# LayerNorm tile by tile, one activation table set for its root, and the first gate chunks multiplied tile by tile

## The chip, the cores and the metric

The kernel runs on one core of a Trainium2 chip. The metric is the device time of one execution in microseconds; three runs of the kernel before gave 2117.9, 2118.01 and 2118.44 us, and their median is what the changed kernel is compared with. The engines are named as the profile names them: PE multiplies matrices (PEld is its weight loading), DVE and ACT work on whole tiles element by element (ACT also evaluates functions such as the logarithm, from tables that an ACT_TABLE_LOAD brings in), POOL is a third elementwise engine, and SP issues most of the DMAs. Each engine executes its own instructions in order and waits for the others by semaphores.

## What is computed

A two-layer decoder trunk over 512 tokens of width 2048. Each layer has a mixer (sparse attention in layer 0, stick-breaking attention in layer 1), and after it the same tail, which is the only part that the change touches:

```
for i in range(DEPTH):                                   # DEPTH = 2
    y = mixer_i(x, ...)                                  # ends with a product with w_out
    x = _layer_norm(DN_ALPHA * x + y, ln_g[i], ln_b[i])  # (x - mu) * rsqrt(var + eps) * g + b
    x = x + (p[i] @ w_ple[i]) * jax.nn.sigmoid(x @ w_ple_gate[i])
```

All arithmetic is float32. The normalised x is the input of the product with `w_ple_gate`, so no gate product can start before the LayerNorm has delivered at least its first tile.

## The kernel before, in words

Activations lie transposed: a tile is 128 features by 512 tokens, and the residual stream is 16 such tiles, here tile 0 to tile 15. To keep float32 accuracy on PE, every factor is split into a high part (a rounded copy, written by ACT) and a low part (the difference, written by DVE), and a product is three matmuls of 512 columns: high weight by high tile (L120), high weight by low tile (L121), low weight by high tile (L122), in `mm3`. The high part of a tile is needed at the first of these, its low part at the second.

Weights come as chunks of 128x1024 numbers (512 KB), one DMA each into one of six `raw` buffers. `split_w` turns a chunk into `wh` (ACT, L294) and `wl` (DVE, L295); there are three pairs of `wh`/`wl` buffers (`HL_BUFS = 3`), and the split of chunk c is issued two chunks ahead, at the start of chunk c-2. `Kernel.run` goes through the list of chunks in order: first `ahead(c)` (splits and loads due), then the chunk's multiplications, then its `after` function, then deferred work. So the place of a call in this list is the place of its instructions in every engine's queue. PSUM gives four banks for products (tag `g`).

The tail of a layer consists of these chunks:

- 32 chunks of `w_out`, which end in the 16 unnormalised tiles `z` and in running sums for the statistics.
- Four `ple` chunks, the product with `w_ple`, of four outputs with 6 matmuls each. ACT copies each output out of PSUM (L851). After the first of them `ln_stats` multiplies the sums by a matrix of ones (L794, L795) and forms mean and variance. When output 5 is out, `ln_rstd` makes the inverse root: a logarithm (L808), an exponential (L809), and one Newton step on DVE (L810 to L813).
- Eight blocks of `w_gate`, each for two output tiles, of four chunks with 8 products (24 matmuls) each; chunk `kc` of a block uses tiles 4kc to 4kc+3. Blocks 0 and 1 are zipped: gate chunk 0 is chunk 0 of block 0, gate chunk 1 is chunk 0 of block 1, gate chunk 2 is chunk 1 of block 0 and so on up to gate chunk 7. So gate chunks 0 and 1 use tiles 0 to 3, gate chunks 2 and 3 use tiles 4 to 7.

`ln_apply` normalises groups of tiles: two DVE operations for each tile (L840 minus the mean, L841 times the root), then scale and offset (on DVE, L843, for tiles 0 to 3; on ACT, L845, for the others), and when this has been issued for the whole group, `k.split` for each (ACT L104 the high part, DVE L105 the low part). Its groups are tiles 0 and 1 (after the third ple chunk), 2 and 3 (at output 13), 4 to 7 (after gate chunk 0), 8 to 11 (after gate chunk 2) and 12 to 15 (after gate chunk 4).

Of the kernel before, what the change touches and what calls it, by code (L numbers as in the profile page):

```python
# [6 lines left out]
F32 = mybir.dt.float32  # L7
F32R = mybir.dt.float32r
I32 = mybir.dt.int32
AF = mybir.ActivationFunctionType  # L10
OP = mybir.AluOpType

P = 128
T = 512
NT = T // P
D = 2048
KT = D // P
# [23 lines left out]
class Out:  # L41
    def __init__(self, n, done, col=0):
        self.col = col
        self.n = n
        self.left = n
        self.done = done
        self.ps = None


class Chunk:  # L50
    def __init__(self, loads, mms, pre=None, after=None, pops=1):
        self.pops = pops
        self.mid = None
        self.parts = 1
        self.between = None
        self.grown = None
        self.add = None
        self.plus = None
        self.product = None
        self.loads = loads  # L60
        self.mms = mms
        self.pre = pre
        self.after = after
# [12 lines left out]
class Kernel:  # L76
# [70 lines left out]
    def zip_last(self):  # L147
        c = self.chunks
        c[-8:] = [c[b] for kc in range(4) for b in (kc - 8, kc - 4)]

    def whole(self, src, n):
        return lambda raw: self.nc.sync.dma_start(raw, src[n])
# [178 lines left out]
    def run(self):  # L331
        self.plan()
        self.prologue()
        for c in range(len(self.chunks)):
            ch = self.chunks[c]
            self.now = c
            if not ch.mid:
                self.ahead(c)
            if ch.pre:
                ch.pre()  # L340
            if ch.product:
                ch.product(ch)
            for n, (off, out, xs) in enumerate(ch.mms):
                if ch.mid and n == len(ch.mms) // 2:
                    ch.mid()
                    self.ahead(c)
                if out.ps is None:
                    out.ps = self.ps("g")
                first = out.left == out.n
                out.left -= 1  # L350
                x = xs()
                if isinstance(off, tuple):
                    a = tuple(z[:, off[1] * P:(off[1] + 1) * P] for z in x)
                    b = tuple(z[:, off[0]:off[0] + T] for z in (ch.h, ch.l))
                else:
                    a = tuple(z[:, off:off + P] for z in (ch.h, ch.l))
                    b = tuple(z[:, out.col:] for z in x)
                self.mm3(out.ps[:, out.col:], a, b, first, out.left == 0)
                if out.left == 0:
                    out.done(out.ps)  # L360
            ch.h = ch.l = None
            if ch.after:
                ch.after()
            self.pop(ch.pops)
            while self.late:
                self.late.pop(0)()
# [15 lines left out]
def _emit(k, xt, pt, positions, lncols, freq, w_in, w_out, w_gate, w_ple, w_kv, w_v, w_q, out):  # L382
    nc, const = k.nc, k.const
# [8 lines left out]
    lncol = const.tile([P, 64], F32, name="lncol")  # L392
# [12 lines left out]
    ones = const.tile([P, P], F32, name="ones")  # L405
# [65 lines left out]
    kidx, qidx, wi_nat, score, bias = {}, {}, {}, {}, {}  # L471
# [86 lines left out]
    xs = lambda m: xT[m]  # L558
# [191 lines left out]
    dT = {}  # L750
    ln = {}
# [40 lines left out]
    def ln_stats():  # L792
        m_ps, e_ps = k.ps("s"), k.ps("s")
        nc.tensor.matmul(m_ps, ones, ln["a1"], start=True, stop=True)  # L794
        nc.tensor.matmul(e_ps, ones, ln["a2"], start=True, stop=True)  # L795
        warm = k.small()
        nc.scalar.activation(warm, ones[:, 0:1], AF.Ln)
        mean, var, r, q = k.tt(s="mean"), k.tt(s="var"), k.tt(s="rstd"), k.tt(s="lnq")
        nc.scalar.copy(mean, m_ps)
        ln["mean"] = mean  # L800
        nc.vector.tensor_tensor(q, mean, mean, op=OP.mult)
        nc.vector.tensor_tensor(var, e_ps, q, op=OP.subtract)
        nc.vector.tensor_scalar(var, var, 0.0, EPS, op0=OP.max, op1=OP.add)
        ln["rstd"], ln["var"], ln["q"] = r, var, q

    def ln_rstd():
        r, var, q = ln["rstd"], ln.pop("var"), ln.pop("q")
        nc.scalar.activation(r, var, AF.Ln)  # L808
        nc.scalar.activation(r, r, AF.Exp, scale=-0.5)  # L809
        nc.vector.tensor_tensor(q, r, r, op=OP.mult)  # L810
        nc.vector.tensor_tensor(q, q, var, op=OP.mult)
        nc.vector.tensor_scalar(q, q, -0.5, 1.5, op0=OP.mult, op1=OP.add)
        nc.vector.tensor_tensor(r, r, q, op=OP.mult)  # L813

    xn = {}
# [17 lines left out]
        f = F[name][j]  # L833
        return f[:, :HALF], f[:, HALF:]

    def ln_apply(layer, ms):
        for m in ms:
            gcol = lncol[:, layer * 16 + m:layer * 16 + m + 1]
            bcol = lncol[:, 32 + layer * 16 + m:32 + layer * 16 + m + 1]
            nc.vector.tensor_tensor(dT[m], dT[m], ln["mean"], op=OP.subtract)  # L840
            nc.vector.tensor_tensor(dT[m], dT[m], ln["rstd"], op=OP.mult)  # L841
            if m < 4:
                nc.vector.tensor_scalar(dT[m], dT[m], gcol, bcol, op0=OP.mult, op1=OP.add)  # L843
            else:
                nc.scalar.activation(dT[m], dT[m], AF.Identity, scale=gcol, bias=bcol)  # L845
        for m in ms:
            xn[m] = k.split(dT[m])

    def ple_done(layer, m, ps):
        t = k.tt(s="ple")  # L850
        nc.scalar.copy(t, ps)  # L851
        pl[m] = t
        if m == 5:
            ln_rstd()
        elif m == 13:
            ln_apply(layer, range(2, 4))

    def ple_chunks(layer):
        for c in range(4):
            outs = [Out(2, lambda ps, m=4 * c + i: ple_done(layer, m, ps)) for i in range(4)]  # L860

            mms = [(kt * 512 + i * P, outs[i], (lambda kt=kt: pT[layer][kt])) for i in range(4) for kt in range(2)]

            ch = Chunk(k.whole(w_ple[layer], c), mms, pre=finish if c == 0 else None)
            ch.pops = 1
            if c == 0:
                ch.after = ln_stats
            elif c == 2:
                ch.after = lambda: ln_apply(layer, range(0, 2))
            k.chunks.append(ch)  # L870

    def mix_out(layer):
# [27 lines left out]
    def halves(m):  # L900
        return (slice(0, 256), slice(256, 512)) if m == KT - 1 else (slice(0, T),)

    def gate_block(layer, fin):
        def done(b, i, ps):
            m = 2 * b + i
            sg = k.tt(s="sg")
            for c in halves(m):
                nc.scalar.activation(sg[:, c], ps[:, c], AF.Sigmoid)
                nc.vector.tensor_tensor(sg[:, c], sg[:, c], pl[m][:, c], op=OP.mult)
                nc.vector.tensor_tensor(sg[:, c], sg[:, c], dT[m][:, c], op=OP.add)  # L910
            pl[m] = dT[m] = None
            fin(m, sg)

        def ahead(kc):
            if kc < 3:
                ln_apply(layer, range(4 * kc + 4, 4 * kc + 8))

        for b in range(KT // 2):
            k.block(w_gate[layer], 4 * b, lambda m: xn[m],
                    lambda i, ps, b=b: done(b, i, ps), pops=1)  # L920
            if b == 1:
                k.zip_last()
                for kc in range(3):
                    k.chunks[2 * kc - 8].after = lambda kc=kc: ahead(kc)

    x1, xd, ud = {}, {}, {}

# [26 lines left out]

    mix_out(0)
    ple_chunks(0)
    gate_block(0, x1_fin)
    for n in range(3):
        k.chunks[n - 4].then(lambda n=n: gate_end(n))
# [101 lines left out]

    mix_out(1)
    ple_chunks(1)
    gate_block(1, out_fin)
    k.run()
    finish()
# [68 lines left out]
```

## Time and profile before

| | |
|---|---|
| median of 3 runs | 2118.01 us |
| lowest, highest | 2117.9, 2118.44 us |
| the profiled execution, its own time | 2118.33 us |
| span of its trace, first to last instruction | 2116.6 us |
| PE busy | 2100.8 us, 99% of the span |
| DVE, ACT, POOL busy | 1346.2, 958.8, 224.5 us |
| mean granted PE clock | 0.998 of full speed |

The difference between 2118.33 and 2116.6 us lies outside the first and the last instruction. The busy time of PE counts matmuls that overlap each other (each is shown longer than the distance to the next one's start), so time is best read from the starts of successive matmuls.

### The profile page before, as it was taken

The page shows a single profiled execution, that of the slowest core. Times are in us where ns is not written, and L with a number is a line of the kernel's source. Part 1 is how long each engine was busy: PE and PEld are TensorE (multiplying, and loading weights), DVE is VectorE, ACT ScalarE, POOL GpSimd, SP SyncE. Part 2 cuts the span into 40 slices and gives each one's busy share as a digit, 9 for nine tenths or more (in the row PEclk, how much of TensorE's full clock was granted, in tenths as well). Part 3 has the DMA queues.
Part 4 walks back from the last instruction along what each step waited for, and adds up shares of the span by engine and source line. Part 5 has one row for each costly group of instructions (what it writes and reads, how often), then busy time and mean ns, then how long its engine had stood idle before and what let it go on. Part 6 is the DMA issues. An engine that isn't in the chain of part 4 may idle for free.

```text
span 2116.6 us, 30578 instructions
## 1 busy us (share of the span) xinstructions
PE 2100.8 (99%) x12160; PEld 1860.5 (88%) x12160; DVE 1346.2 (64%) x2048; ACT 958.8 (45%) x1513; POOL 224.5 (11%) x287
## 2 busy tenths in 40 slices
PE   9999999999999999999999999999999999999999
PEld 7987888888888887888899999999999998887887
DVE  5577966556565447634777777777777775437533
ACT  4564355445553226423555554545555553226421
POOL 5201000000001100000011111111111100100000
PEclk9999999999999999999999999999999999999999
DMA  6332222222223332433455554555554563332331
GB/s 244 100 100 80 100 80 80 80 70 77 75 98 130 120 111 78 132 117 121 119 129 134 145 156 127 154 154 134 155 152 125 148 228 118 120 119 80 130 120 40
DMA packets 77759, 252.89 MB, mean 119 GB/s; under 512 B 8880, under 2 KB 9136, under 8 KB 77616
## 3 DMA queue, kind: packets, MB, share of 16 engines
q1 hardware_dynamic: 68976, 219.48, 30.1%
q0 software_dynamic: 8640, 31.46, 8.5%
q8 instruction: 95, 1.56, 0.3%
q14 instruction: 48, 0.39, 0.1%
HBM read 238.85 MB, written 12.06 MB: 119 GB/s over the span
## 4 chain that ended last, share of the span: by engine, by line
PE 92%; DVE 3%; issue 2%; ACT 1%; POOL 0%; DMA 0%; SPq 0%; POOLq 0%; DVEq 0%; ACTq 0%
PE g L179 26%; PE g L120 19%; PE g L121 19%; PE g L122 19%; PE s L579 2%; PE o L121 1%; PE o L122 1%; PE o L120 1%; PE s L120 1%; PE s L121 1%; PE s L122 1%; PE s L513 1%; DVE wl L295 1%; DVE z L841 1%; DVE z L840 0%
## 5 line engine op out<-in xcount | busy, mean ns | idle before, releaser
L295 DVE TENSOR_TENSOR wl<-raw,wh 128x1024 fp32r<-128x1024 f32 (+1 forms) x453 | 558.2, 1237 | 387.7 <-ACT wh L294 385.3
L120 PE MATMUL g<-h,wh 128*128 128x512 f32 (+1 forms) x1808 | 702.9, 389 | 3.4 <-ACT h L104 3.4
L121 PE MATMUL g<-l,wh 128*128 128x512 f32 (+1 forms) x1808 | 698.8, 387 | 3.2 <-DVE l L105 3.2
L122 PE MATMUL g<-h,wl 128*128 128x512 f32 (+1 forms) x1808 | 698.2, 386 | 0.5 <-DVE wl L295 0.5
L294 ACT CAST wh<-raw 128x1024 fp32r<-128x1024 f32 (+1 forms) x453 | 473.1, 1049 | 397.6 <-PE g L121 266.9
L179 PE MATMUL g<-f,wh 128*128 128x256 f32 x3360 | 619.4, 284 | 0.0
L179 PEld LDWEIGHTS g<-f,wh 128*128 128x128 f32 x3360 | 528.6, 192 | 0.8
L179 PE MATMUL g<-f,wl 128*128 128x256 f32 x1680 | 475.5, 283 | 2.0 <-DVE wl L295 2.0
L120 PEld LDWEIGHTS g<-h,wh 128*128 128x128 f32 x1808 | 340.1, 188 | 74.4 <-ACT h L104 4.9
L121 PEld LDWEIGHTS g<-l,wh 128*128 128x128 f32 x1808 | 340.2, 188 | 69.6 <-DVE l L105 4.8
L122 PEld LDWEIGHTS g<-h,wl 128*128 128x128 f32 x1808 | 340.2, 188 | 67.0 <-DVE wl L295 1.0
L179 PEld LDWEIGHTS g<-f,wl 128*128 128x128 f32 x1680 | 322.1, 192 | 3.6 <-DVE wl L295 2.9
L278 POOL DMA_DIRECT2D raw<-in_w_q_dram x60 | 53.1, 1041 | 591.2 <-issue 279.4
L637 ACT ACTIVATE pr<-pr,s 128x128 f32<-128x128 f32 (+1 forms) x64 | 36.1, 563 | 126.5 <-DVE s L636 126.1
L461 POOL TENSOR_TENSOR rb<-rb,sin 128x512 f32<-128x512 f32 (+2 forms) x29 | 35.9, 1237 | 470.2 <-ACT rb L459 317.7
L790 POOL TENSOR_TENSOR a<-a,sq 128x512 f32<-128x512 f32 x30 | 40.4, 1345 | 331.2 <-ACT sq L788 331.0
L283 DVE TENSOR_TENSOR raw<-raw,raw 128x1024 f32<-128x1024 f32 x60 | 73.1, 1219 | 0.0
L105 DVE TENSOR_TENSOR l<-s,h 128x512 fp32r<-128x512 f32 (+1 forms) x108 | 60.0, 605 | 18.4 <-ACT h L104 18.4
L652 DVE TENSOR_TENSOR_SCAN r<-keep,zeros 128x127 f32<-128x127 f32 (+1 forms) x64 | 54.4, 850 | 13.7 <-POOL keep L649 13.7
L104 ACT CAST h<-s 128x512 fp32r<-128x512 f32 (+1 forms) x108 | 50.2, 531 | 25.9 <-PE s L1006 13.4
L462 DVE TENSOR_TENSOR ra<-ra,cos 128x512 f32<-128x512 f32 (+2 forms) x29 | 32.7, 1129 | 36.1 <-ACT ra L460 36.0
L645 ACT ACTIVATE keep<-s 128x128 f32<-128x128 f32 (+1 forms) x64 | 28.1, 439 | 53.6 <-PE s L122 53.6
(179 smaller groups left out, 1916.5 us busy)
## 6 DMA issues: line engine op xcount, KB each, us to landing
raw<-in_w_in_dram SPq DMA_DIRECT2D x97, 512.0 KB, 3.3
raw<-in_w_out_dram SPq DMA_DIRECT2D x64, 512.0 KB, 3.3
raw<-in_w_gate_dram SPq DMA_DIRECT2D x64, 512.0 KB, 3.3
raw<-in_w_q_dram SPq DMA_DIRECT2D x64, 512.0 KB, 5.3
raw<-in_w_q_dram POOLq DMA_DIRECT2D x60, 512.0 KB, 6.5
raw<-in_w_kv_dram SPq DMA_DIRECT2D x56, 512.0 KB, 3.8
xin<-in_x_dram SPq DMA_DIRECT2D x16, 256.0 KB, 6.0
x<-in_x_dram SPq DMA_DIRECT2D x16, 256.0 KB, 3.7
```

Of the source, the lines that this page charges most:

```text
L104: nc.scalar.copy(h[:, lo:w], src[:, lo:w])
L105: nc.vector.tensor_tensor(l[:, lo:w], src[:, lo:w], h.bitcast(F32)[:, lo:w], op=OP.subtract)
L120: nc.tensor.matmul(out, ah, bh, start=start, stop=False)
L121: nc.tensor.matmul(out, ah, bl, start=False, stop=False)
L122: nc.tensor.matmul(out, al, bh, start=False, stop=stop)
L179: nc.tensor.matmul(ps[:, :HALF], a, b, start=start and j == 0 and n == 0, stop=stop and j == KT // 2 - 1 and n == 2, skip_group_check=True)
L278: self.nc.gpsimd.dma_start(ch.raw, ch.add, accum_op=OP.add)
L283: self.nc.vector.tensor_tensor(ch.raw, ch.raw, ch.plus.raw, op=OP.add)
L294: nc.scalar.copy(ch.h[:, i:i + w], ch.raw[:, i:i + w])
L295: nc.vector.tensor_tensor(ch.l[:, i:i + w], ch.raw[:, i:i + w], ch.h.bitcast(F32)[:, i:i + w], op=OP.subtract)
L579: nc.tensor.transpose(banks[b][:, off + (i - j) * P:off + (i - j + 1) * P], a["p"][i][:, j * P:(j + 1) * P], ident)
L652: nc.vector.tensor_tensor_scan(r[:, 0:n - 1][:, ::-1], keep[:, 1:n][:, ::-1], zeros.to_broadcast([P, n - 1]), 1.0, op0=OP.mult, op1=OP.add)
```

## The change

The logarithm no longer follows a dummy activation that pulls in a table set; one table set that holds logarithm and exponential is loaded by name, once in each layer's tail. `ln_apply` is replaced by `ln_norm` (the two DVE operations), `ln_high` (scale and offset, on DVE for tiles 0 and 1 only, then the high part) and `ln_low` (the low part); `ln_tiles` issues for each tile m: `ln_high(m)`, `ln_norm(m + 1)`, `ln_low(m)`. The places of the calls change too: `ln_norm(0)` right behind the root, tile 0 at output 12, tile 1 at output 14, tiles 2 to 4 after the fourth ple chunk, tiles 5 to 7 after gate chunk 0, then two tiles each after gate chunks 1, 2, 3 and 4.

`merge_last(8)` empties gate chunk 0 of its multiplications and gives them to gate chunk 1, two of the one and two of the other in turn; gate chunk 0 keeps its weights (`held`) until gate chunk 1 is done. The multiplications of all eight chunks are sorted by tile. The numbers of lines grow by 1 in `mm3`, by 8 in `split_w` and by about 12 further down.

```diff
+    def merge_last(self, n):
+
+        a, b = self.chunks[-n], self.chunks[len(self.chunks) - n + 1]
+        a.held = True
+        b.mms = [(*m, ch) for i in range(0, len(a.mms), 2) for ch in (a, b) for m in ch.mms[i:i + 2]]
+        a.mms = []
...
-        warm = k.small()
-        nc.scalar.activation(warm, ones[:, 0:1], AF.Ln)
+        nc.scalar.preload_act_table_set("natural_log_exp_and_others")
...
+    def ln_norm(m):
+        nc.vector.tensor_tensor(dT[m], dT[m], ln["mean"], op=OP.subtract)
+        nc.vector.tensor_tensor(dT[m], dT[m], ln["rstd"], op=OP.mult)
+
+    def ln_high(layer, m):
+        gcol = lncol[:, layer * 16 + m:layer * 16 + m + 1]
+        bcol = lncol[:, 32 + layer * 16 + m:32 + layer * 16 + m + 1]
+        if m < 2:
+            nc.vector.tensor_scalar(dT[m], dT[m], gcol, bcol, op0=OP.mult, op1=OP.add)
+        else:
+            nc.scalar.activation(dT[m], dT[m], AF.Identity, scale=gcol, bias=bcol)
+        xn[m] = k.tt(F32R, "h"), k.tt(F32R, "l")
+        nc.scalar.copy(xn[m][0], dT[m])
+
+    def ln_low(m):
+        h, l = xn[m]
+        nc.vector.tensor_tensor(l, dT[m], h.bitcast(F32), op=OP.subtract)
+
+    def ln_tiles(layer, lo, hi):
+
+        for m in range(lo, hi):
+            ln_high(layer, m)
+            if m + 1 < KT:
+                ln_norm(m + 1)
+            ln_low(m)
...
         if m == 5:
             ln_rstd()
-        elif m == 13:
-            ln_apply(layer, range(2, 4))
+            ln_norm(0)
+        elif m in (12, 14):
+            ln_tiles(layer, m // 2 - 6, m // 2 - 5)
...
-            elif c == 2:
-                ch.after = lambda: ln_apply(layer, range(0, 2))
+            elif c == 3:
+                ch.after = lambda: ln_tiles(layer, 2, 5)
...
                 k.zip_last()
-                for kc in range(3):
-                    k.chunks[2 * kc - 8].after = lambda kc=kc: ahead(kc)
+                for ch in k.chunks[-8:]:
+                    ch.mms.sort(key=lambda m: m[0])
+                k.merge_last(8)
+                k.chunks[-8].after = lambda: ln_tiles(layer, 5, 8)
+                for n in range(4):
+                    k.chunks[n - 7].after = lambda n=n: ln_tiles(layer, 2 * n + 8, 2 * n + 10)
```

How the instructions of layer 0 stand now is shown at three places. The first is PE at the start of the gate product. Before, `g_7041` and `g_7045` are the two outputs of gate chunk 0, `wh_6923` and `wl_6924` its weights, `h_6971`, `l_6972` tile 0 and `h_6975`, `l_6976` tile 1:

```order
L120 MATMUL g_7041<-h_6971,wh_6923 128x512
L121 MATMUL g_7041<-l_6972,wh_6923 128x512
L122 MATMUL g_7041<-h_6971,wl_6924 128x512
L120 MATMUL g_7045<-h_6971,wh_6923 128x512
L121 MATMUL g_7045<-l_6972,wh_6923 128x512
L122 MATMUL g_7045<-h_6971,wl_6924 128x512
L120 MATMUL g_7041<-h_6975,wh_6923 128x512
L121 MATMUL g_7041<-l_6976,wh_6923 128x512
L122 MATMUL g_7041<-h_6975,wl_6924 128x512
L120 MATMUL g_7045<-h_6975,wh_6923 128x512
```

In the change `g_7076` and `g_7080` are the outputs of gate chunk 0, `g_7084` and `g_7088` those of gate chunk 1, `wh_6924` and `wh_6966` their weights, `h_6982` is tile 0 and `h_7007` tile 1:

```order
L121 MATMUL g_7076<-h_6982,wh_6924 128x512
L122 MATMUL g_7076<-l_6983,wh_6924 128x512
L123 MATMUL g_7076<-h_6982,wl_6925 128x512
L121 MATMUL g_7080<-h_6982,wh_6924 128x512
L122 MATMUL g_7080<-l_6983,wh_6924 128x512
L123 MATMUL g_7080<-h_6982,wl_6925 128x512
L121 MATMUL g_7084<-h_6982,wh_6966 128x512
L122 MATMUL g_7084<-l_6983,wh_6966 128x512
L123 MATMUL g_7084<-h_6982,wl_6967 128x512
L121 MATMUL g_7088<-h_6982,wh_6966 128x512
L122 MATMUL g_7088<-l_6983,wh_6966 128x512
L123 MATMUL g_7088<-h_6982,wl_6967 128x512
```

The matmuls of gate chunk 1 have moved up, so that each of tiles 0 to 3 is used by 12 matmuls before the next tile is touched, where it was 6. The second place is PE at gate chunk 2, which brings in tiles 4 to 7 (before `h_7079`, `h_7083`, `h_7087`, `h_7091`):

```order
L120 MATMUL g_7041<-h_7079,wh_7035 128x512
L121 MATMUL g_7041<-l_7080,wh_7035 128x512
L122 MATMUL g_7041<-h_7079,wl_7036 128x512
L120 MATMUL g_7041<-h_7083,wh_7035 128x512
L121 MATMUL g_7041<-l_7084,wh_7035 128x512
L122 MATMUL g_7041<-h_7083,wl_7036 128x512
L120 MATMUL g_7041<-h_7087,wh_7035 128x512
L121 MATMUL g_7041<-l_7088,wh_7035 128x512
```

In the change the first tiles of this chunk are `h_7037` and `h_7050`:

```order
L121 MATMUL g_7076<-h_7037,wh_7043 128x512
L122 MATMUL g_7076<-l_7038,wh_7043 128x512
L123 MATMUL g_7076<-h_7037,wl_7044 128x512
L121 MATMUL g_7080<-h_7037,wh_7043 128x512
L122 MATMUL g_7080<-l_7038,wh_7043 128x512
L123 MATMUL g_7080<-h_7037,wl_7044 128x512
L121 MATMUL g_7076<-h_7050,wh_7043 128x512
L122 MATMUL g_7076<-l_7051,wh_7043 128x512
```

Gate chunk 2 touches a new tile every 6 matmuls, where it was every 3. The third place is DVE, from the split of gate chunk 2's weights on. Before, tiles 4 to 7 (`z_6093`, `z_6112`, `z_6233`, `z_6252`) follow it as one group, and their four low parts stand behind all eight operations:

```order
L295 TENSOR_TENSOR wl_7036<-raw_6823,wh_7035 128x1024
L840 TENSOR_TENSOR z_6093<-z_6093,mean_6867 128x512
L841 TENSOR_TENSOR z_6093<-z_6093,rstd_6869 128x512
L840 TENSOR_TENSOR z_6112<-z_6112,mean_6867 128x512
L841 TENSOR_TENSOR z_6112<-z_6112,rstd_6869 128x512
L840 TENSOR_TENSOR z_6233<-z_6233,mean_6867 128x512
L841 TENSOR_TENSOR z_6233<-z_6233,rstd_6869 128x512
L840 TENSOR_TENSOR z_6252<-z_6252,mean_6867 128x512
L841 TENSOR_TENSOR z_6252<-z_6252,rstd_6869 128x512
L105 TENSOR_TENSOR l_7080<-z_6093,h_7079 128x512
L105 TENSOR_TENSOR l_7084<-z_6112,h_7083 128x512
```

In the change, from the low part of tile 3 (`l_7031`) on:

```order
L864 TENSOR_TENSOR l_7031<-z_5944,h_7030 128x512
L849 TENSOR_TENSOR z_6112<-z_6112,mean_6866 128x512
L850 TENSOR_TENSOR z_6112<-z_6112,rstd_6868 128x512
L864 TENSOR_TENSOR l_7038<-z_6093,h_7037 128x512
L303 TENSOR_TENSOR wl_7044<-raw_6823,wh_7043 128x1024
L849 TENSOR_TENSOR z_6233<-z_6233,mean_6866 128x512
L850 TENSOR_TENSOR z_6233<-z_6233,rstd_6868 128x512
L864 TENSOR_TENSOR l_7051<-z_6112,h_7050 128x512
L849 TENSOR_TENSOR z_6252<-z_6252,mean_6866 128x512
L850 TENSOR_TENSOR z_6252<-z_6252,rstd_6868 128x512
L864 TENSOR_TENSOR l_7058<-z_6233,h_7057 128x512
```

The low part of a tile now follows the two operations of the next tile, and the split of gate chunk 2's weights (`wl_7044`) stands behind tile 4 instead of ahead of it. On ACT the second ACT_TABLE_LOAD (L809, between logarithm and exponential) and the dummy activation (L797) are gone in each layer, and the scale and offset of tiles 2 and 3 are added. The order of the DMAs on SP and of the work on POOL is the same in both kernels.

## Rows read from the trace of the kernel before

**Rows 1.** The head of the page: the span, and busy time, share and instructions of each engine.

```profile
span 2116.6 us, 30578 instructions
PE 2100.8 (99%) x12160; PEld 1860.5 (88%) x12160; DVE 1346.2 (64%) x2048; ACT 958.8 (45%) x1513; POOL 224.5 (11%) x287
```

**Rows 2.** The waits of PE over the whole span: line, the engine and line waited for, us in total, times, the longest.

```profile
PE g L120 <- ACT h L104: 3.4, 2, 1.7
PE g L121 <- DVE l L105: 3.2, 4, 1.4
PE g L179 <- DVE wl L295: 2.0, 4, 0.6
...
```

**Rows 3.** The timeline of PE at gate chunk 0 of layer 0: start, duration, instruction, and in brackets the idle time before it with its releaser. The first row is the first gate matmul, the second the last one that uses tile 1.

```profile
819.00 0.39 PE L120 MATMUL g<-h,wh 128*128 128x512 f32 x1
...
821.50 0.39 PE L122 MATMUL g<-h,wl 128*128 128x512 f32 x1
821.79 0.50 PE L120 MATMUL g<-h,wh 128*128 128x512 f32 x1
823.64 0.50 PE L121 MATMUL g<-l,wh 128*128 128x512 f32 x1 [1.35 <-DVE l L105]
...
824.21 0.39 PE L120 MATMUL g<-h,wh 128*128 128x512 f32 x1
```

**Rows 4.** The same view at gate chunk 2 of layer 0. The first row is the last matmul of gate chunk 1; the last row is the 13th matmul after it.

```profile
831.47 0.39 PE L122 MATMUL g<-h,wl 128*128 128x512 f32 x1
833.54 0.50 PE L120 MATMUL g<-h,wh 128*128 128x512 f32 x1 [1.69 <-ACT h L104]
...
834.61 0.41 PE L122 MATMUL g<-h,wl 128*128 128x512 f32 x1
...
838.49 0.39 PE L120 MATMUL g<-h,wh 128*128 128x512 f32 x1
```

**Rows 5.** The same two places in layer 1, in the same view: the last matmul ahead of a wait, the matmul that waited, and the 4th or 13th matmul after the first of them.

```profile
1934.16 0.39 PE L122 MATMUL g<-h,wl 128*128 128x512 f32 x1
...
1936.32 0.50 PE L121 MATMUL g<-l,wh 128*128 128x512 f32 x1 [1.35 <-DVE l L105]
...
1936.89 0.40 PE L120 MATMUL g<-h,wh 128*128 128x512 f32 x1
...
1944.16 0.39 PE L122 MATMUL g<-h,wl 128*128 128x512 f32 x1
1946.21 0.50 PE L120 MATMUL g<-h,wh 128*128 128x512 f32 x1 [1.66 <-ACT h L104]
...
1951.15 0.39 PE L120 MATMUL g<-h,wh 128*128 128x512 f32 x1
```

**Rows 6.** Stretches of layer 0 around the two waits: the stretch, its length, busy time of each engine with its number of instructions, then the granted PE clock (1.00 is full speed, 2.4 GHz), the DMA share and GB/s.

```profile
819.00:831.70 12.70, 11.35 (x49) 8.74 (x47) 11.11 (x18) 5.61 (x8) 0.00 (x0) 1.00 0.24 83
831.70:840.00 8.30, 6.39 (x20) 4.76 (x20) 6.87 (x10) 5.01 (x8) 0.00 (x0) 0.79 0.22 66
840.00:865.00 25.00, 25.00 (x112) 20.69 (x111) 20.88 (x31) 17.35 (x25) 0.00 (x0) 1.00 0.28 94
```

**Rows 7.** The timeline of DVE in layer 0, from the Newton step of the root to the low parts of tiles 4 to 7; columns as in rows 3.

```profile
808.75 0.69 DVE L810 TENSOR_TENSOR lnq<-rstd 128x512 f32<-128x512 f32 x1 [1.94 <-ACT rstd L809]
...
811.27 1.22 DVE L295 TENSOR_TENSOR wl<-raw,wh 128x1024 fp32r<-128x1024 f32 x1
812.41 0.68 DVE L840 TENSOR_TENSOR z<-z,mean 128x512 f32<-128x512 f32 x1
...
813.85 0.55 DVE L843 TENSOR_SCALAR z<-z,lncol 128x512 f32<-128x512 f32 x1
814.31 0.68 DVE L840 TENSOR_TENSOR z<-z,mean 128x512 f32<-128x512 f32 x1
...
826.74 0.68 DVE L840 TENSOR_TENSOR z<-z,mean 128x512 f32<-128x512 f32 x1
827.46 0.69 DVE L841 TENSOR_TENSOR z<-z,rstd 128x512 f32<-128x512 f32 x1
828.07 0.68 DVE L840 TENSOR_TENSOR z<-z,mean 128x512 f32<-128x512 f32 x1
...
833.52 2.50 DVE L105 TENSOR_TENSOR l<-z,h 128x512 fp32r<-128x512 f32 x4 [1.39 <-ACT h L104]
```

**Rows 8.** The timeline of ACT in the same stretch: the root with its table load, the copy of ple output 11 and what follows it, the split of gate chunk 1's weights, scale and offset of tile 7, and the high parts of tiles 4 to 7.

```profile
806.14 0.63 ACT L808 ACTIVATE rstd<-var 128x512 f32<-128x512 f32 x1
806.79 1.28 ACT L809 ACT_TABLE_LOAD   x1
808.09 0.63 ACT L809 ACTIVATE rstd<-rstd 128x512 f32<-128x512 f32 x1
...
813.76 0.59 ACT L851 COPY ple<-g 128x512 f32<-128x512 f32 x1 [0.72 <-PE g L122]
814.49 0.62 ACT L104 CAST h<-z 128x512 fp32r<-128x512 f32 x1
...
816.87 1.05 ACT L294 CAST wh<-raw 128x1024 fp32r<-128x1024 f32 x1
...
832.17 0.81 ACT L845 ACTIVATE z<-z,lncol 128x512 f32<-128x512 f32 x1 [0.51 <-DVE z L841]
832.89 2.16 ACT L104 CAST h<-z 128x512 fp32r<-128x512 f32 x4
```

More of the change, by code (lines that the diff above doesn't have):

```diff
@@ L54, in __init__ @@
         self.parts = 1
+        self.held = False
         self.between = None
@@ L342, in run @@
                 ch.product(ch)
-            for n, (off, out, xs) in enumerate(ch.mms):
+            for n, (off, out, xs, *other) in enumerate(ch.mms):
                 if ch.mid and n == len(ch.mms) // 2:
@@ L346, in run @@
                     self.ahead(c)
+                src = other[0] if other else ch
                 if out.ps is None:
@@ L353, in run @@
                     a = tuple(z[:, off[1] * P:(off[1] + 1) * P] for z in x)
-                    b = tuple(z[:, off[0]:off[0] + T] for z in (ch.h, ch.l))
+                    b = tuple(z[:, off[0]:off[0] + T] for z in (src.h, src.l))
                 else:
-                    a = tuple(z[:, off:off + P] for z in (ch.h, ch.l))
+                    a = tuple(z[:, off:off + P] for z in (src.h, src.l))
                     b = tuple(z[:, out.col:] for z in x)
@@ L360, in run @@
                     out.done(out.ps)
-            ch.h = ch.l = None
+            if not ch.held:
+                ch.h = ch.l = None
+            for m in ch.mms:
+                if len(m) > 3:
+                    m[3].h = m[3].l = None
             if ch.after:
@@ L834, in form @@
         return f[:, :HALF], f[:, HALF:]
[L836 to L847, printed above, removed]
+    def ln_norm(m):
[19 more added lines that the diff above has]
+            ln_low(m)
     def ple_done(layer, m, ps):
@@ L912, in done @@
             fin(m, sg)
-        def ahead(kc):
-            if kc < 3:
-                ln_apply(layer, range(4 * kc + 4, 4 * kc + 8))
         for b in range(KT // 2):
```

## The prediction

> **What bounds the kernel now.** The head of the page comes first: PE is busy for 2100.8 of 2116.6 us [rows 1], so a change that leaves the matmuls alone can only win back what PE waits, and what it runs at a lower clock. The waits of PE come next [rows 2]: 3.4 us for ACT at L104 and 3.2 us for DVE at L105, the high and low parts of activation tiles. The timeline puts them at two places in each layer. At gate chunk 0 the matmul with the low part of tile 2 waits 1.35 us for DVE [rows 3]; at gate chunk 2 the first matmul with tile 4 waits 1.69 us for ACT [rows 4]. Layer 1 shows the same with 1.35 and 1.66 us [rows 5].
>
> A wait costs more than its idle time, so I count by starts. Without a wait, 11 spacings take 821.50 - 819.00 = 2.50 us [rows 3], 0.227 us each. Four spacings from 821.50 should take 0.91 us and take 2.71: 1.80 lost. Thirteen from 831.47 should take 2.95 and take 7.02: 4.07 lost [rows 4]. Of these, 3.88 - 10 x 0.227 = 1.61 us lie behind 834.61, when nothing is waited for: the granted clock is 0.79 of full speed in this stretch and 1.00 before and after [rows 6], so part of it ran at 1.2 GHz, right behind the two waits. In layer 1 the losses are 2.73 - 0.91 = 1.82 and 6.99 - 2.95 = 4.04 us [rows 5]. The sum is 11.73 us, 0.55% of the time; this is all that the change can win here.
>
> **The change part by part.** No matmul and no DMA is added or removed, and the queues of SP and POOL stand as before; the loads (512 KB each) are not touched. What changes is when a tile is due on PE and when ACT and DVE deliver it.
>
> *Due times.* I take the start of the first gate matmul, 819.00 [rows 3], as fixed: PE has no wait in the ple chunks ahead of it. Before, without any wait, tile 2 would be due 12 spacings later, at 821.73, and tiles 4 to 7 from 48 spacings on at 829.89, 830.57, 831.25 and 831.93. In the change tiles 1, 2 and 3 are due 12 spacings apart, at 821.73, 824.45 and 827.17, and tiles 4 to 7 six apart, at 829.89, 831.25, 832.61 and 833.97. The low part is due one spacing (0.23) later than the high part.
>
> *Delivery.* The root's table: between logarithm and exponential lies a load of 1.28 us, and the exponential starts 1.30 us after the load [rows 8]. Without it the root and `ln_norm(0)` move up by 1.30: DVE's Newton step starts at 807.45 instead of 808.75 [rows 7], the root is there at about 810.0, tile 0's two operations end at 811.3, and the split of gate chunk 0 (1.14) at 812.5. Then DVE must wait anyway: next stands the low part of gate chunk 1's weights, whose high part ACT starts only behind the copy of ple output 11 (813.76 + 0.49 = 814.25, 1.05 us long) [rows 8]. So DVE goes on at 815.33. The 2.8 us of this wait cover the table load; with the load kept, DVE would reach the wait at 813.8 and the end would be the same. I cost this part at nothing; without that cover it would be worth 1.30 us a layer.
>
> From 815.33 on DVE runs through. Prices, from start to next start [rows 7]: a weight split 812.41 - 811.27 = 1.14, scale and offset of tile 0 or 1 0.46, the two operations of a tile 828.07 - 826.74 = 1.33, a low part 0.61 (four take 2.50, the last of them 0.69). The low part of tile 0 starts at 815.33 + 1.14 + 0.46 + 1.33 = 818.26 and ends at 818.95; due 819.23. Tile 1: 0.61 + 0.46 + 1.33 = 2.40 later, 821.35; due 821.96. Tiles 2, 3, 4 at 0.61 + 1.33 = 1.94 each: 823.29, 825.23, 827.17; due 824.68, 827.40, 830.12. The split of gate chunk 2 (1.14) comes in here, so tile 5 is ready at 830.25 (due 831.48), tile 6 at 832.19 (due 832.84), tile 7 at 834.13 (due 834.20). ACT keeps up: for each tile scale and offset (0.81) and the high part (0.62) [rows 8] run one behind the other while DVE does 1.94, and the next tile's two operations stand on DVE ahead of the low part that waits for ACT. This is also what removes the 1.39 us that DVE waited for ACT ahead of the four low parts [rows 7].
>
> *What is queued behind.* The merged chunk keeps two of the three weight buffers, so the split for gate chunk 3 must wait for its end at 829.89. On ACT and DVE it stands behind tile 7 anyway: ACT at about 833.0 to 834.0, DVE 834.06 to 835.29; gate chunk 3 starts at 835.33 and wants the low weights two spacings later, 835.78. From then on DVE needs 2 x 1.94 + 1.14 = 5.02 us for each chunk and PE 24 x 0.227 = 5.44, and tile 8 is ready at about 837.2 for 840.8. PSUM: the fourth bank is wanted 9 spacings after 819.00, at 821.05; the copy that empties it stands on ACT behind tile 1's high part (ready to start at 819.5) and ends at about 820.6. The two outputs of a zipped block now end together and the two evictions queue, but the next block's banks are due more than 5 us later.
>
> So on paper every wait goes, with margins of 0.07 us (tile 7), 0.28 (tile 0) and 0.5 (weights of chunk 3) at the tightest. These are sums over 18 us of DVE work, good to a few tenths, and lateness does not add up: a stall gives all later tiles the same respite, so a layer pays about its largest one. I leave 0.3 us a layer for it. 11.73 - 0.6 = 11.1; 2118.33 - 11.1 = 2107.2 for an execution like the profiled one, which lies 0.3 us above the median: **2106.9 us**.
>
> **The rivals.** No change is anything within 0.2%, 4.2 us, which is about what these runs can tell apart.
>
> *Left-over waits and the clock.* The clock fell behind waits of 1.35 and 1.69 us that lay 10 us apart; after the first alone it did not [rows 3, 4, 6]. If tile 7 is 0.7 us late and the clock falls all the same, a layer pays 0.7, some 0.2 for the restart (rows 3 lose 1.80 on 1.35 idle), and 1.6: 2.5, 5.0 for both, 2118.0 - 11.7 + 5.0 = 2111.3 us. For it speaks the margin of 0.07; against it the single wait that left the clock alone. The Trainium skill, "TensorE: Matmul & The Clock Gate", section "A second HAM failure mode: psum-queue depth-cycling", says that short idle times between groups of matmuls can make the clock swing between its two levels; that speaks against a change that trades two long waits for a row of tight due times. By that rule alone the clock's 3.2 us in the two layers would stay, about 2110; the trace has only one pattern to show, and it needed both waits.
>
> *The waits come back as late tiles.* If ACT's two operations are not hidden behind the next tile's DVE work, every tile costs up to 1.39 us more on DVE, the wait ahead of the batched low parts [rows 7]. At half of it, 0.7 a tile over tiles 2 to 7, tile 7 is 4.2 us late and the clock falls as before (1.6): 5.8 a layer, all that was won, 2118 us. Against it: 0.81 + 0.62 is less than 1.94.
>
> *Slower: three weight buffers.* The merged chunk holds two, so splits can no longer run ahead. If every split of gate chunks 3 to 7 were exposed behind the matmuls that free its buffer, PE would wait 1.05 + 1.23 us [rows 7, 8], five times: 11.4 a layer, 22.8 in all, 2118 - 11.7 + 22.8 = 2129 us. It decides from (11.7 + 4.2) / 2 = 8 us a layer on, 1.6 us for each split. Against it: after 829.89 each split has a whole chunk of 5.44 us, and DVE needs 5.02.
>
> **How the numbers follow.** The waits go (2105.7 to 2108.5; the low end is nothing left and 0.6 us of spread): 0.72. Left-over waits and the clock (2108.5 to 2113.8): 0.14. Waits come back, no change: 0.08. Slower: 0.06. Faster by over 0.2% is the first two, 0.86. The range for 8 in 10 is 2105.7 to 2110.8: the first case and the better part of the second.
>
> **What the profile of the changed kernel would show.** Right: no wait of PE over 0.5 us in the gate chunks; granted clock 1.00 where it was 0.79; PE's idle time down by about 6 us, its busy time by 3 to 4 (matmuls at the lower clock are shown longer); DVE without a gap from 815.3 to about 834, its wait ahead of that being for gate chunk 1's high weights and not for the root. Wrong: a wait of PE for DVE at tile 5, 6 or 7 or for `wl` at gate chunk 3, or a stretch at the lower clock without a wait. The prediction fails most easily by ACT: if its copies and high parts run late at tile 0 or 1, everything behind them on DVE shifts, and tile 7 has no margin to take it.

## The result, and the profile after

The changed kernel takes 2106.86 us (median of 6 runs, 2106.46 to 2107.78), the kernel before 2118.23 us beside it (6 runs, 2117.9 to 2118.56). The ratio is 0.9947 with an interval from 0.9934 to 0.9959: faster by 11.4 us. The forecast was 2106.9 us. Later times are medians too; in one run, e3_pe_order, two of the eleven executions took 2728.04 and 7418.19 us, far from all others, and are left out of its median.

The head of the page of the changed kernel, and the waits of PE over its whole span (line, engine and line waited for, us in total, times, longest), to be held against [rows 1, 2]. The lines of the matmuls with high tile, low tile and low weight are now L121, L122 and L123:

```profile
span 2106.1 us, 30574 instructions
PE 2097.0 (100%) x12160; PEld 1860.3 (88%) x12160; DVE 1341.6 (64%) x2044; ACT 960.6 (46%) x1513; POOL 225.0 (11%) x287
```

```profile
PE g L187 <- DVE wl L303: 1.9, 4, 0.5
PE o L703 <- POOL ident L400: 1.4, 1, 1.4
PE g L123 <- DVE wl L303: 0.5, 1, 0.5
PE g L121 <- ACT wh L302: 0.3, 1, 0.3
```

The 3.4 us for ACT's high parts and the 3.2 us for DVE's low parts are gone; what is left lies in other stages. The stretches of [rows 6] in the changed kernel (length, busy time of PE, PEld, DVE, ACT, POOL with instructions, granted clock, DMA share, GB/s):

```profile
819.00:831.70 12.70, 12.70 (x57) 10.52 (x57) 12.53 (x20) 9.35 (x15) 0.00 (x0) 1.00 0.18 65
831.70:840.00 8.30, 8.30 (x38) 6.69 (x37) 8.16 (x13) 6.50 (x9) 0.00 (x0) 1.00 0.22 80
```

PE is busy throughout, where it was busy for 11.35 and 6.39 us, and the clock is 1.00 where it was 0.79. DVE is busy for 12.53 of 12.70 us: it now runs without a gap. Its timeline in layer 0, with the four splits up to gate chunk 3's, and the low parts of tiles 0 and 7:

```profile
812.49 1.22 DVE L303 TENSOR_TENSOR wl<-raw,wh 128x1024 fp32r<-128x1024 f32 x1
816.50 1.23 DVE L303 TENSOR_TENSOR wl<-raw,wh 128x1024 fp32r<-128x1024 f32 x1 [2.79 <-ACT wh L302]
...
819.43 0.68 DVE L864 TENSOR_TENSOR l<-z,h 128x512 fp32r<-128x512 f32 x1
...
828.25 1.22 DVE L303 TENSOR_TENSOR wl<-raw,wh 128x1024 fp32r<-128x1024 f32 x1
...
834.58 0.68 DVE L864 TENSOR_TENSOR l<-z,h 128x512 fp32r<-128x512 f32 x1
835.22 1.23 DVE L303 TENSOR_TENSOR wl<-raw,wh 128x1024 fp32r<-128x1024 f32 x1
836.37 0.68 DVE L849 TENSOR_TENSOR z<-z,mean 128x512 f32<-128x512 f32 x1
...
841.41 0.68 DVE L849 TENSOR_TENSOR z<-z,mean 128x512 f32<-128x512 f32 x1
```

The last two rows are one chunk's worth of DVE work apart (two tiles and a split): 5.04 us.

This execution runs 1.17 us behind the profiled one of before (the last section shows where that comes from): its first gate matmul starts at 820.17, where it was 819.00. On PE there is one place left, the first matmul with tile 7's low part:

```profile
820.17 0.39 PE L121 MATMUL g<-h,wh 128*128 128x512 f32 x1
...
835.36 0.46 PE L122 MATMUL g<-l,wh 128*128 128x512 f32 x1
835.65 0.39 PE L123 MATMUL g<-h,wl 128*128 128x512 f32 x1
```

From 835.36 to 835.65 are 0.29 us where a spacing is 0.227, and DVE ends that low part at 834.58 + 0.68 = 835.26. This 0.06 us, with some hundredths around it 0.08, is all that either layer still loses in its gate chunks.

### The profile page after: what moved, and what is told of

Same layout as the page of the kernel before. It is cut to its first block, busy times and chain, and to the rows that moved or that the text cites. A ratio compares the mean times of both kernels' runs of the same rounds, so it can differ in the third digit from the quotient of the medians.

```text
span 2106.1 us, 30574 instructions
## 1 busy us (share of the span) xinstructions
PE 2097.0 (100%) x12160; PEld 1860.3 (88%) x12160; DVE 1341.6 (64%) x2044; ACT 960.6 (46%) x1513; POOL 225.0 (11%) x287
## 4 chain that ended last, share of the span: by engine, by line
PE 95%; issue 2%; DVE 1%; ACT 1%; POOL 0%; DMA 0%; SPq 0%; POOLq 0%; DVEq 0%; ACTq 0%
PE g L187 26%; PE g L121 20%; PE g L123 20%; PE g L122 20%; PE s L592 2%; PE o L122 1%; PE o L123 1%; PE o L121 1%; PE s L121 1%; PE s L122 1%; PE s L123 1%; PE s L526 1%; DVE r L665 0%; DVE wl L303 0%; POOL keep L662 0%
## 5 line engine op out<-in xcount | busy, mean ns | idle before, releaser
L121 PE MATMUL g<-h,wh 128*128 128x512 f32 (+1 forms) x1808 | 701.6, 388 | 0.0
L123 PE MATMUL g<-h,wl 128*128 128x512 f32 (+1 forms) x1808 | 697.7, 386 | 0.5 <-DVE wl L303 0.5
L122 PE MATMUL g<-l,wh 128*128 128x512 f32 (+1 forms) x1808 | 697.6, 386 | 0.0
L121 PEld LDWEIGHTS g<-h,wh 128*128 128x128 f32 x1808 | 339.6, 188 | 69.0 <-issue 3.4
L123 PEld LDWEIGHTS g<-h,wl 128*128 128x128 f32 x1808 | 339.5, 188 | 66.4 <-DVE wl L303 1.0
L122 PEld LDWEIGHTS g<-l,wh 128*128 128x128 f32 x1808 | 339.7, 188 | 65.7 <-issue 0.5
```

Source lines behind the costliest of these rows:

```text
L121: nc.tensor.matmul(out, ah, bh, start=start, stop=False)
L122: nc.tensor.matmul(out, ah, bl, start=False, stop=False)
L123: nc.tensor.matmul(out, al, bh, start=False, stop=stop)
```

## The experiments

My theory was the one of the prediction: the time won is that of the waits, each wait is a tile's due time on PE against its delivery by DVE, and the change needs both sides, the later due times and the earlier delivery. The rivals: the table set gives a part; the order on PE alone, or the delivery alone, gives all; short waits bring the clock down. The kernel before took 2118.51 us (median) beside the first four runs and 2118.52 us beside the last four, 0.3 us more than beside the changed kernel; a difference of that size between two runs means nothing.

**e1_two_loads: the changed kernel with two table loads.**

```diff
-        nc.scalar.preload_act_table_set("natural_log_exp_and_others")
+        warm = k.small()
+        nc.scalar.activation(warm, ones[:, 0:1], AF.Ln)
```

> The changed kernel with the dummy logarithm back in place of the named table set, so that logarithm and exponential load a table each, as before the change. My theory: the load between them (1.28 us in the trace of before) is covered, because DVE waits anyway, 2.79 us in the trace of the changed kernel, for the high weights of gate chunk 1, and all later work hangs on that; the time stays at 2106.9 us within 0.5, and that wait of DVE shrinks to about 1.4 us. Rival, the root's table load is a part of the gain: 1.3 us in each layer by the trace, 2109.5 us. The Trainium skill (ScalarE: Activation LUTs, section What ACT_TABLE_LOAD costs) gives a switch of table sets 2.66 us with a drain; by that figure alone the rival would be at 2112.2 us.

Measured: 2106.91 us (2106.53 to 2107.91), 0.05 us from the changed kernel's median. ACT in this run, logarithm, load and exponential, and DVE at the split of gate chunk 1's weights:

```profile
806.07 0.63 ACT L821 ACTIVATE rstd<-var 128x512 f32<-128x512 f32 x1
806.72 1.28 ACT L822 ACT_TABLE_LOAD   x1
808.02 0.63 ACT L822 ACTIVATE rstd<-rstd 128x512 f32<-128x512 f32 x1
```

```profile
812.53 1.22 DVE L303 TENSOR_TENSOR wl<-raw,wh 128x1024 fp32r<-128x1024 f32 x1
815.26 1.23 DVE L303 TENSOR_TENSOR wl<-raw,wh 128x1024 fp32r<-128x1024 f32 x1 [1.51 <-ACT wh L302]
```

DVE's wait shrinks from 2.79 to 1.51 us and covers the load. In this order of the work the table set is worth nothing that these runs can tell.

**e2_one_set: the kernel before with the table set alone.**

```diff
-        warm = k.small()
-        nc.scalar.activation(warm, ones[:, 0:1], AF.Ln)
+        nc.scalar.preload_act_table_set("natural_log_exp_and_others")
```

> The kernel before with the named table set alone; order of the work and of the matmuls as before. My theory: here nothing covers the load, since DVE ran without a gap from the root to the low part of tile 2; the chain moves up by 1.30 us, the first wait of each layer loses 1.35 of its 1.80 us, and the second stays at tile 4, since PE arrives there earlier by as much as the tiles do. If the clock falls behind the second wait alone, 2118.2 - 2.7 = 2115.5 us. If the fall needs the first wait too, another 3.2 us go: 2112.3 us. By the 2.66 us that the Trainium skill (ScalarE: Activation LUTs, section What ACT_TABLE_LOAD costs) states for a switch, the whole first wait would go: about 2114.6 us.

Measured: 2115.62 us (2115.38 to 2116.6), 2.9 below the kernel before: the total that I gave for the case with the fall of the clock, but not by that case. PE in layer 0 at gate chunk 2, and at the first low parts of tiles 8 and 12; then the stretch around the first:

```profile
831.37 0.39 PE L122 MATMUL g<-h,wl 128*128 128x512 f32 x1
833.41 0.50 PE L120 MATMUL g<-h,wh 128*128 128x512 f32 x1 [1.65 <-ACT h L104]
...
845.73 0.50 PE L121 MATMUL g<-l,wh 128*128 128x512 f32 x1 [0.23 <-DVE l L105]
...
857.31 0.50 PE L121 MATMUL g<-l,wh 128*128 128x512 f32 x1 [0.23 <-DVE l L105]
```

```profile
831.70:842.00 10.30, 8.43 (x37) 6.68 (x36) 8.79 (x13) 6.42 (x9) 0.00 (x0) 1.00 0.33 101
```

The first wait shrank to 0.26 us, the second is as long as before (1.65 for 1.69), and the clock stays at 1.00, so 1.6 us more should have gone in each layer. Most of it comes back at tiles 8 and 12: the matmuls around each lose 0.7 us by starts, and these waits are not in the trace of before. All in all the layers lose 4.3 and 4.4 us by starts, where it was 5.87 and 5.86; of this 1.5 us the table load accounts for 1.3. What sets the pace there is DVE, whose groups of four tiles follow each other at 11.58 us in this run:

```profile
838.19 0.68 DVE L839 TENSOR_TENSOR z<-z,mean 128x512 f32<-128x512 f32 x1
...
849.77 0.68 DVE L839 TENSOR_TENSOR z<-z,mean 128x512 f32<-128x512 f32 x1
```

PE needs 48 x 0.227 = 10.9 us for the two chunks that use a group. So from tile 4 to tile 12 DVE sets the pace of this kernel and of the one before, and the slow matmuls behind the fall only hid it there.

**e3_pe_order: the kernel before with the new order on PE alone** (`merge_last` is as in the change).

```diff
...
                 k.zip_last()
+                for ch in k.chunks[-8:]:
+                    ch.mms.sort(key=lambda m: m[0])
+                k.merge_last(8)
```

> The kernel before with the new order on PE alone (chunks sorted by tile, gate chunks 0 and 1 merged); LayerNorm in groups and two table loads as before. My theory: the wait at tile 2 goes, since tile 2 is then due at 824.45 and its low part is there at 823.6, but tile 4 still comes at 833.5 for 829.89, so the one wait left is 3.65 us instead of 1.84 and takes back what the other gave: 5.1 to 5.9 us are lost in each layer, where it was 5.87; 2117.3 us, at most 1.6 below before. Rival, the order of the matmuls is what removes the waits: 2107 to 2110 us.

Measured: 2118.7 us, ratio to before 1.0 (0.9991 to 1.0009): no change, about as the theory has it, but the wait is elsewhere. PE in layer 0 from the first gate matmul on, ACT there, and the stretch around the wait:

```profile
819.10 0.39 PE L121 MATMUL g<-h,wh 128*128 128x512 f32 x1
...
820.23 0.39 PE L123 MATMUL g<-h,wl 128*128 128x512 f32 x1
824.29 0.79 PE L121 MATMUL g<-h,wh 128*128 128x512 f32 x1 [3.67 <-ACT ple L864]
```

```profile
823.14 0.62 ACT L105 CAST h<-z 128x512 fp32r<-128x512 f32 x1 [1.29 <-DVE z L856]
823.66 1.07 ACT L864 COPY ple<-g 128x512 f32<-128x512 f32 x2
```

```profile
819.00:831.70 12.70, 9.03 (x34) 7.02 (x33) 11.11 (x18) 5.53 (x8) 0.00 (x0) 0.87 0.27 83
```

The matmul that waits for 3.67 us is the 7th of the gate product (819.10 to 820.23 are five spacings), the first into the third PSUM bank; the copy that empties this bank, the first of the last two, stands on ACT behind tile 3's high part, which waits for DVE. Merging two chunks makes all four banks due within 2 us. The clock fell behind this wait (0.87 between 819.0 and 831.7); with it the layer lost 5.7 us, nearly as much as before.

**e5_pe_order_bank: the same, with the bank free in time.**

```diff
-        elif m == 13:
-            ln_apply(layer, range(2, 4))
...
+            elif c == 3:
+                ch.after = lambda: ln_apply(layer, range(2, 4))
```

> The new order on PE alone, as in the run e3_pe_order, with one more edit: the high parts of tiles 2 and 3 are issued behind the last copy of a ple output, not ahead of the last two. In that run PE waited 3.67 us not at tile 4 but at the 10th gate matmul, for the PSUM bank that this copy empties. My theory: the bank was only the first of two limits; with it free by 820 PE runs on and waits at tile 4, whose high part is still there at 833.5 only, for 829.89; 4.3 us lost there, 1.3 more by a fall of the clock or, without a fall, by waits at tiles 8 and 12, since DVE then sets the pace; 2117.8 us. Rival, the bank was the limit and the order on PE is what removes the waits: 2107 to 2112 us.

Measured: 2116.4 us (ratio 0.999, 0.9981 to 0.9999), 2.1 us below the kernel before. (The matmul that waited for the bank was the 7th, not the 10th.) The bank was the first of two limits: PE now waits at tile 4, in both layers, and the two layers differ in one thing. The first two rows and the first stretch are layer 0, the rest is layer 1:

```profile
829.79 0.39 PE L123 MATMUL g<-h,wl 128*128 128x512 f32 x1
832.73 0.50 PE L121 MATMUL g<-h,wh 128*128 128x512 f32 x1 [2.54 <-ACT h L105]
...
1941.52 0.39 PE L123 MATMUL g<-h,wl 128*128 128x512 f32 x1
1944.46 0.50 PE L121 MATMUL g<-h,wh 128*128 128x512 f32 x1 [2.56 <-ACT h L105]
...
1956.77 0.50 PE L122 MATMUL g<-l,wh 128*128 128x512 f32 x1 [0.23 <-DVE l L106]
...
1968.36 0.50 PE L122 MATMUL g<-l,wh 128*128 128x512 f32 x1 [0.22 <-DVE l L106]
```

```profile
831.70:842.00 10.30, 9.05 (x32) 7.08 (x32) 9.18 (x13) 6.46 (x10) 0.00 (x0) 0.83 0.27 103
...
1944.00:1956.00 12.00, 11.32 (x48) 8.94 (x48) 10.03 (x14) 7.66 (x12) 0.00 (x0) 1.00 0.28 89
```

In layer 0 the clock fell (0.83) and tiles 8 and 12 came in time; in layer 1 it did not (1.00) and PE waited at both. By starts the layers lost 4.9 and 4.7 us: with DVE setting the pace the fall costs next to nothing. The wait at tile 4 is shorter than the 3.65 us expected, 2.94 - 0.23 = 2.7, because the edit also took two copies out of ACT's way to the split of gate chunk 2's weights, which starts at 823.70 here and at 824.62 in e3_pe_order; 0.92 us in each layer are more than the 1.4 us by which I was off.

**e4_tiles_only: the changed kernel without the new order on PE.**

```diff
                 k.zip_last()
-                for ch in k.chunks[-8:]:
-                    ch.mms.sort(key=lambda m: m[0])
-                k.merge_last(8)
```

> The changed kernel without the new order on PE: LayerNorm tile by tile and one table set as in the change, gate chunks neither sorted nor merged. My theory: tiles 1, 2 and 3 are due 6 matmuls (1.36 us) apart while DVE delivers one in 1.94 to 2.40 us, so three short waits come at tiles 1 to 3, 1.9 us and some restarts together, 2.1 to 2.4 us in each layer; after them PE is late enough that tiles 4 to 7 arrive in time. 2106.9 + 4.5 = 2111.4 us, and 2114.6 us if the clock falls behind them in both layers. Rival, the delivery tile by tile is the whole gain and the order on PE adds nothing: 2107 us.

Measured: 2110.79 us (2110.27 to 2112.21), 3.9 above the changed kernel. The waits stand where they should, at the low parts of tiles 1, 2 and 3, and lose 2.0 us by starts in each layer; the clock stays at 1.00:

```profile
821.37 0.50 PE L122 MATMUL g<-l,wh 128*128 128x512 f32 x1 [0.62 <-DVE l L864]
...
823.30 0.50 PE L122 MATMUL g<-l,wh 128*128 128x512 f32 x1 [0.27 <-DVE l L864]
...
825.23 0.51 PE L122 MATMUL g<-l,wh 128*128 128x512 f32 x1 [0.27 <-DVE l L864]
```

The parts of the new delivery (the order of the calls, the place of the split, scale and offset of tiles 2 and 3 on ACT) were not run one by one.

**e8_merge_only: the changed kernel merged, but not sorted.**

```diff
-                for ch in k.chunks[-8:]:
-                    ch.mms.sort(key=lambda m: m[0])
```

> The changed kernel with gate chunks 0 and 1 merged, but without sorting the other six by tile. My theory: tiles 0 to 3 have their 12 matmuls each and come in time, tiles 4 to 7 are due 3 matmuls (0.68 us) apart; tile 6 is 0.75 us late and tile 7 another 1.1, 2.0 to 2.2 us with the restarts in each layer: 2111 us. Rival, merging is what matters and sorting adds nothing: 2106.9 us.

Measured: 2111.05 us (2110.69 to 2112.61), 4.2 above the changed kernel. Tiles 0 to 3 come in time, tiles 6 and 7 do not, and each layer loses 2.1 us:

```profile
832.54 0.50 PE L122 MATMUL g<-l,wh 128*128 128x512 f32 x1 [0.53 <-DVE l L864]
...
834.47 0.51 PE L122 MATMUL g<-l,wh 128*128 128x512 f32 x1 [0.53 <-DVE l L864]
```

So the merge without the sort gives nothing against e4_tiles_only: the 2 us of lateness that it removes at tiles 1 to 3 come up at tiles 6 and 7, since a late PE had given those tiles their time. The sort without the merge was not run.

**e6_late1 and e7_late3: the changed kernel with DVE made late by a known amount** (one and three operations; the edit shown is that of e7_late3):

```diff
             ln_high(layer, m)
+            if m == 5:
+                for _ in range(3):
+                    nc.vector.tensor_tensor(ln["mean"], ln["mean"], ln["mean"], op=OP.max)
```

> The changed kernel with one more DVE operation of 128x512 in each layer, ahead of the two operations of tile 6 (the mean against itself, which leaves it as it is). My theory of due times: 0.72 us later on DVE use up the margin of tile 6 (0.65) and overdraw that of tile 7 (nothing); PE pays 0.8 to 0.9 us in each layer where it was 0.08, and the clock stays at 1.00: 2108.5 us. Rival, a short wait makes the clock fall: 1.6 us more in each layer, 2111.7 us. Rival, the margin is larger than I worked out: 2106.9 us.

> The changed kernel with three such DVE operations, 2.16 us, ahead of tile 6. My theory: tile 5 is 0.9 us late, tiles 6 and 7 take three short waits' sum to 2.2 or 2.3 us in each layer, no more, since lateness does not add up; the clock stays: 2111.4 us. Rival, the waits make the clock fall: 2114.6 us. Rival, each of the three late tiles pays its own lateness (0.9 + 1.5 + 2.2 = 4.6 us): 2116 us.

Measured: 2108.36 us (2108.09 to 2109.63) and 2111.72 us (2110.64 to 2112.57), with 0.77 and 2.21 us lost by starts in each layer. The waits of e7_late3 in layer 0, at tiles 5, 6 and 7, and the stretch around them:

```profile
833.04 0.50 PE L122 MATMUL g<-l,wh 128*128 128x512 f32 x1 [0.83 <-DVE l L864]
...
834.97 0.50 PE L122 MATMUL g<-l,wh 128*128 128x512 f32 x1 [0.27 <-DVE l L864]
...
836.90 0.51 PE L122 MATMUL g<-l,wh 128*128 128x512 f32 x1 [0.28 <-DVE l L864]
```

```profile
831.70:842.00 10.30, 8.92 (x37) 6.40 (x36) 10.16 (x16) 7.74 (x11) 0.00 (x0) 1.00 0.14 52
```

2.16 us of delay leave a layer with 2.21 us lost, not with the sum of three latenesses, and 0.72 us leave it with 0.77; 0.08 were lost without any delay. The clock stays at full speed behind waits of 0.83, 0.27 and 0.28 us.

## Why the prediction was right, and where it was not

**The sum.** 11.73 us of loss were read from the trace of before, 0.6 were left for remaining stalls. The changed kernel loses 2 x 0.08 = 0.17 us, so 11.56 were won where the medians show 11.37. The 0.6 was too careful; the profiled execution's smaller gain (2116.6 - 2106.1 = 10.5 us of span) is its later start, 1.17 us. PE's idle time fell by 6.7 us and its busy time by 3.8, as forecast. That the median came out within 0.1 us is in part luck: the gain was 0.27 us larger than the 11.1 forecast, and the kernel before was 0.22 us slower beside it than the median that the forecast started from.

**Due times and delivery.** This step carried the number, and it held to a few hundredths. With the 1.17 us of later start taken off, DVE goes on at 816.50 - 1.17 = 815.33 (worked out: 815.33), tile 0's low part ends at 818.94 (818.95), tile 7's at 834.09 (834.13), gate chunk 3's split starts at 834.05 (834.06). The tightest margin was given for tile 7, and tile 7 is the one place where PE still loses time. e6_late1 and e7_late3 confirm the margins: lateness put in by hand is paid once it exceeds them, and once for all later tiles.

**The table load at nothing.** Right, with the cover that was named: with two loads the time is the same (2106.91 us in e1_two_loads), and DVE's wait for the high weights takes up the load. Without the cover, in the order of before, the set is worth 2.9 us (e2_one_set), 1.45 a layer. The Trainium skill ("ScalarE: Activation LUTs", section "What ACT_TABLE_LOAD costs") gives each switch 2.66 us, 1283 ns of load and a drain. The trace agrees on the load (1.28 us) and leaves no room for a drain: the exponential starts 808.02 - 806.07 = 1.95 us after the logarithm with the load and 807.98 - 807.31 = 0.67 us after it in the changed kernel, 1.28 us apart.

**The clock.** This is the step that failed, without harm to the sum. I booked 1.61 us of each layer's 4.07 to the lower clock, as time that comes back when the clock does not fall. e2_one_set and the two layers of e5_pe_order_bank show that with DVE's old pace nearly all of it stays lost: DVE delivered a group of four tiles in 11.6 us and PE used it in 10.9, so without the fall PE waits at tiles 8 and 12 instead. I had compared these two paces for the change (5.02 against 5.44 a chunk) and not for the kernel before, where the rows gave them too: 833.52 + 2.50 - 826.74 = 9.28 us and two splits of 1.14 [rows 7]. The gain came all the same because the change took DVE's 1.39 us of waiting out of each group: now two chunks' worth of DVE work takes 2 x 5.04 = 10.1 us. My expectation for e2_one_set hit its total by the wrong branch for the same reason. That the fall needs two waits, as I read the one pattern of before, is not so either: in both layers of e3_pe_order and in layer 0 of e5_pe_order_bank it came behind one.

**The rivals.** Left-over waits that bring the clock down: not seen, neither in the changed kernel nor with waits of up to 0.83 us put in. The rule quoted with it (the Trainium skill, "TensorE: Matmul & The Clock Gate", section "A second HAM failure mode: psum-queue depth-cycling") does not show for these short waits. Waits that come back as late tiles: not seen; the next tile's two operations hide ACT, and from 816.50 to 853 DVE does not wait once. Three weight buffers: gate chunk 3's split starts at 835.22, behind the end of the merged chunk and before PE wants it; no wait of PE for `wl` is left in the gate chunks. That a change of PE's order alone would move the wait, here to a PSUM bank, was not among the rivals; the prediction had only checked the fourth bank's due time (821.05, emptied at 820.6) for the change as it is. It held: the copy ends at 821.19 + 0.58 = 821.77 there, with the 1.17 us taken off at 820.60. e3_pe_order shows that the banks had to be checked.

## What to carry to other kernels

Where one engine feeds another tile by tile, write down for each tile when it is due and when it is there, from start-to-start times of the trace; the largest lateness is what is paid, and it falls both by delivering earlier and by using each tile longer before the next one. Price either half of such a change alone too: here the order on PE alone gave nothing (2.1 us once its bank was free in time), the delivery alone two thirds. And before booking a lower clock as a loss, compare the pace of the engine that feeds it: here that was slower anyway, and the layer with the fall lost 4.9 us, the one without it 4.7.

## What the runs showed of the hardware

A fall of the clock does not follow from the length of a wait alone. It came behind 1.35 and 1.69 us in the kernel before, behind 3.67 us alone in e3_pe_order and 2.54 us alone in layer 0 of e5_pe_order_bank, and not behind 2.56 us in layer 1 of the same execution, nor behind 1.65 us in e2_one_set. What tells these cases apart the runs do not show.

The start of an execution is not the same each time. In the profiled one of the changed kernel the matmuls behind the first weights follow each other at nearly twice the usual distance:

```profile
5.39 0.79 PE L121 MATMUL g<-wh,h 128*128 128x512 f32 x1 [0.30 <-ACT wh L302]
...
6.71 0.63 PE L123 MATMUL g<-wh,l 128*128 128x512 f32 x1
7.14 0.63 PE L121 MATMUL g<-wh,h 128*128 128x512 f32 x1
```

The last two starts lie 0.43 us apart, and this goes on for some 3 us. In the kernel before this distance went with a granted clock of 0.50 (835.20 to 838.20, inside the stretch at 0.79); here the view gives 1.00 from 5.00 to 10.00, so that it was the clock is not shown. In the profiled execution of e1_two_loads, whose code is the same there, the starts are 0.23 us apart from 6.20 on, and its span is 2104.8 us against 2106.1:

```profile
6.20 0.40 PE L123 MATMUL g<-wh,l 128*128 128x512 f32 x1
6.43 0.39 PE L121 MATMUL g<-wh,h 128*128 128x512 f32 x1
```

By the 41st of these matmuls the two are 16.78 - 15.59 = 1.19 us apart, and they stay so up to 50 us. So about a microsecond between two executions is decided in the first 17.
